# Moving a job's masks behind the final transposes, and a projection from the inverse into the carry, in a hybrid RWKV-7 and attention layer

## The chip, the cores and the metric

The kernel runs on one core of one Trainium2 chip. The metric is device time in microseconds (us) of one execution; the time before is the median of three runs.

## The reference

One layer of a diffusion backbone works on two groups of tokens, 512 latent tokens (a grid of width 64) and 128 context tokens, 640 in all, with a model width of 1024, in float32. What matters for the change is the RWKV-7 branch:

```python
h = _rmsnorm(x, p["norm1_g"]) * (1.0 + sc1) + sh1
u_rw, u_na, gate_rw, gate_na = jnp.split(h @ p["w_in"], IN_SPLITS, axis=-1)
...
u = u + mu[0] * (prev - u) + mu[1] * (nxt - u)          # centred shift in time
r, k, v, wd, ad, gd = jnp.split(u, RW_SPLITS, axis=-1)
...
def _wkv_step(s, inp):                                   # forward and backward, 8 heads of 64
    r, w, k, v, a, b = inp
    sa = jnp.einsum("bhvk,bhk->bhv", s, a)
    s = s * w[:, :, None, :] + sa[..., None] * b[:, :, None, :] + v[..., None] * k[:, :, None, :]
    return s, jnp.einsum("bhvk,bhk->bhv", s, r)
...
merged = (jax.nn.sigmoid(gate_rw) * (o_rw @ p["w_o_rwkv"])
          + jax.nn.sigmoid(gate_na) * (o_na @ p["w_o_na"]))
```

Each of r, k and v is a projection of h, shifted in time with its neighbours. The scan is computed in chunks of 64 tokens, which needs for each chunk the inverse of a triangular 64 x 64 matrix. After the branch come the output projection and a feed-forward block, which the change leaves alone.

## The kernel before

Tokens lie along the free dimension (640), channels along the partitions. The RWKV width of 512 is worked through in four channel tiles of 128, that is two heads at a time (`ct` 0 to 3). A tile has 20 lines: 10 chunks of 64 tokens in each of two directions, lines 0 to 9 forward and 10 to 19 backward. Lines 0 to 7 and 12 to 19 belong to the latent tokens, 8 to 11 to the context tokens.

A tile goes through these stages:
- `main`: for all lines the product of AG (the normalised keys with their decay) and BK gives the triangular matrices Nt (L1125).
- `inv`: DVE inverts all 20 lines at once. It transposes 32 x 32 blocks into RL, does 30 elimination steps `s` on them (L1235 to L1253), and transposes the result twice, into RT (L1262) and T (L1264). PE then multiplies with them (L1273, L1287), ACT and DVE copy the result into Rt (L1281, L1292). In steps named by `PRM["jobs"]` three jobs are put in, each for one part of the lines: `v_job` and `t_job` transpose v and BK with small matmuls (L1172, L1195), and `g_job` multiplies BK with AG and R_ (L1144, L1147; L1184 flips v for the backward lines). What a `g_job` leaves in PSUM is masked by DVE in a later step named by `PRM["mds"]`: two multiplications into AG (L1156) and two into TG (L1159). A later `g_job` for lines 12 to 19 reads v lines that the job for lines 0 to 7 has written.
- `carry`: eight slots `s` pass the state from chunk to chunk, in three phases each: AG times ZV (L1321) and a copy x0 by ACT; Rt times x0 (L1348) and a copy into ZV by ACT; TG times ZV (L1361, L1378) and a product with the decay into ZV by DVE (L1373), on which the next slot waits.
- `out`: normalisation, bonus and gating of the tile; it is woven into the next tile's inverse.

All this is latency, so PE's large matmuls are woven in. A queue of units, in the order of `PRM["order"]`, yields one fill matmul at a time (L196): k, r and v of the four tiles, 16 gates g, three low-rank projections l, then the merges a and b. Each of k, r, v, l and g has 48 matmuls, in two halves of 24. `PRM["plan"]` states for each yield of each stage how many fill matmuls follow it. The plan's stages here are inverses of 37 yields and carries of 26. PE, ACT, DVE and GpSimd run in the order that the program writes; only SyncE's order is chosen by the scheduler.

What follows a half is delayed by `later` and counted down by `tick`, one for a fill matmul and two for a yield. A gate's half is followed by a tanh on ACT and a DMA. A projection's first half is followed by a copy into the tile U, its second by another copy (`u_out`) and by the shift: an ACT operation and two DVE operations (L521, L523) for the context's 128 tokens and the same for the latent 512. U has one buffer in this stage, and its memset on GpSimd (L506) opens each projection.

During a carry the due work is held (`hold`) and given out by `beside`, which takes for each yield a budget of ACT and DVE time: work that is due goes first, then steps of `prep` for the next tile (decays, NK, BK: L599 to L688). At slot 7, `last` drains what is left of `prep`, asks for r and v of the next tile, and forms its AG (L1104) and R_ (L1107). Units wait for marks: r of a tile for the bonus of the tile before (`R`), v for the end of its inverse (`I`), k for `M`, set in `last`.

Weights come in float32 and are split into a high part by ACT (L170) and a low part, here on GpSimd in four pieces (L175).

Of the kernel before, what the change touches and what calls it, by code (L numbers as in the profile page):

```python
# [24 lines left out]
TCARGS = dict(schedule_with_timeline_sim=True)  # L25

PRM = dict(
    order=("l0 l1 k0 r0 v0 l2 g0 g1 g2 k1 g3 r1 g4 g5 v1 g6 g7 k2 r2 g8 g9 v2 g10 g11 k3 r3 g12 g13 v3 g15 g14 a0 a1 a2 a3 a4 a5 a6 a7 "
     "b0 b1 b2 b4 b3 b5 b6 b7"),
    plan=(  # L30
        "22.0 0.0 2.0 4.0",
        ("0.0.0 2.0.0 2.0.1 10.0.0 2.0.0 2.0.1 2.0.1 2.0.1 2.0.1 2.0.1 10.0.0 2.0.0 2.0.0 10.0.0 2.0.0 2.0.0 "
# [35 lines left out]
        "w >hb >lb",  # L68
        ""),
    fp=(6, 12, 18), h2e="dpddddpddd", x0e="a", ze="aa", y2=1, y1=0, sc=3, sr=3, sp=1, mg=1.915, h1=0.952,  # L70
    h2=0.91, jobs=((2, 9, 16), (2, 9, 16), (2, 9, 16), (2, 11, 16)),
    mds=((4, 11, 19), (4, 11, 19), (4, 11, 19), (4, 13, 19)), bud=((1.8, 0.8), (1.3, 1.8)), off=6, tk=2, h3=1,
    h4=1.07, g1=2, km="dddddddd", kb="ddpd", ma="d", yo="pppp", r0="pd", rl=(0, 0, 0), lh=(0, 0, 1, 1),
    wl="dddddddddppppppppppppppppppppppppppdpppppppppppp", nu=9, na=(
        "6.0.12.0.1 6.0.12.0.0 6.0.12.0.0 6.0.12.0.2 6.0.12.0.0 6.0.12.0.2 6.0.12.0.0 6.0.12.0.2 6.0.12.0.0 "
        "6.0.12.0.2 6.0.12.1.0 6.1.12.1.2 6.2.12.2.0 6.1.12.2.2 6.0.12.2.0 6.1.12.1.2 6.2.14.2.0 "
        "6.2.14.1.2 6.2.14.2.0 6.2.14.2.0 6.3.18.2.0 10.0.10.0.0"))
# [24 lines left out]
def V(ap, dims, off=0):  # L102

    return bass.AP(ap.tensor, ap.offset + off, [list(ap.ap[0])] + [list(d) for d in dims])
# [3 lines left out]
def body(ctx: ExitStack, tc: tile.TileContext, xs, xp, cols, consts, w_ada, b_row, w_rw, w_qkv,  # L108
# [26 lines left out]
    def nm(s):  # L135
        cn[0] += 1
        return f"{s}_{cn[0]}"
# [8 lines left out]
    def col(n, i=0, rows=slice(0, P)):  # L146
        return C[rows, CO[n] + i:CO[n] + i + 1]
# [40 lines left out]
    def feat_gen(ps, chunk, act_hl, nk, t0, t1, width=128, wcol=0, k0=0):  # L188

        hi, lo = chunk  # L190
        xh, xl = act_hl
        n = 0
        for kt in range(nk):
            a = kt * width + wcol
            for (w, x) in ((hi, xh), (hi, xl), (lo, xh)):
                pe.matmul(ps[:, :t1 - t0], w[:, a:a + 128], x[:, k0 + kt, t0:t1],  # L196
                          start=n == 0, stop=n == 3 * nk - 1)
                n += 1
                yield
# [90 lines left out]
    def dcol(o, i=0, rows=slice(0, P)):  # L290
        return D[rows, o + i:o + i + 1]
# [183 lines left out]
    pend, off, hold = [], [0], [False]  # L475

    def later(fn, cost=(0.5, 0), more=0):
        if off[0]:
            pend.append([off[0] + more, cost, fn])
        else:  # L480
            fn()
# [21 lines left out]
    def proj_gen(ci, out, ps_, usb, utag, ubufs, w):  # L503
        U = usb.tile([P, 643], F32, tag=utag, bufs=ubufs, name=nm("U"))
        pool.memset(V(U[:, :], [[513, 2]]), 0.0)
        pool.memset(U[:, 642:643], 0.0)  # L506
        ps0 = ps_()
        yield from feat_gen(ps0, w, (hh, hl), 8, 0, H2)
        later(lambda: act.copy(U[:, 1:321], ps0[:, :H2]))
        ps1 = ps_()  # L510
        yield from feat_gen(ps1, w, (hh, hl), 8, H2, NT)

        def u_out():
            act.copy(U[:, 321:513], ps1[:, 0:192])
            act.copy(U[:, 514:642], ps1[:, 192:320])  # L515

        def shift(a, b, u):
            o = out[:, a:b]
            n = b - a
            act.activation(o, U[:, u:u + n], AF.Identity, scale=dcol(dm, ci))  # L520
            dve.scalar_tensor_tensor(out=o, in0=U[:, u - 1:u - 1 + n], scalar=col("mu0", ci),  # L521
                                     in1=o, op0=ALU.mult, op1=ALU.add)
            dve.scalar_tensor_tensor(out=o, in0=U[:, u + 1:u + 1 + n], scalar=col("mu1", ci),  # L523
                                     in1=o, op0=ALU.mult, op1=ALU.add)

        later(u_out, (0.6, 0))
        later(lambda: shift(512, 640, 514), (0.4, 0.7), 2)
        later(lambda: shift(0, 512, 1), (0.8, 1.5), 5)

    def proj_shift(ci, out, ps_, usb, utag, ubufs):  # L530
        for _ in proj_gen(ci, out, ps_, usb, utag, ubufs, wload(w_rw[ci])):
            pass
# [159 lines left out]
    gtag = ["fl"]  # L692

    def lora_gen(i, w):

        yield from proj_gen(12 + i, lg_, flps, sb, "U", len(gtag), w)

        def two(d):
            rr, ro = slice(64 * d, 64 * d + 64), slice(64 - 64 * d, 128 - 64 * d)
            act.copy(LX[i][d][rr, :], lg_[rr, :])  # L700
            dve.tensor_tensor(out=LX[i][d][ro, :], in0=lg_[rr, :], in1=LX[i][d][rr, :].bitcast(F32),
                              op=ALU.subtract)

        if i == 2:
            later(lambda: act.activation(lg_, lg_, AF.Tanh, scale=0.5), (0.8, 0), 8)
            later(lambda: dve.tensor_scalar(out=lg_, in0=lg_, scalar1=0.5, scalar2=0.5, op0=ALU.mult, op1=ALU.add),
                  (0, 0.5), 12)
            return
        if i == 0:
            later(lambda: act.activation(lg_, lg_, AF.Tanh), (0.8, 0), 8)  # L710
        for d in range(2):
            later(lambda d=d: two(d), (0.8, 0.8), 12 + 6 * d)
# [6 lines left out]
    def unit(g, e):  # L719

        i, eng = int(g[1:]), eng_of(e)
        if g[0] in "ab":
            return 24 if g[0] == "a" else 18, lambda: merge_load(g[0], i), \
                lambda wt: merge_cast(*wt, eng), lambda w: merge_gen(g[0], i, w)
        if g[0] == "g":
            return 48, lambda: wdma(w_rw[15 + i]), lambda w: wcast(w, eng), \
                lambda w: gate_gen(i, w, flps, sb, gtag[-1])
        ci, dst = {"k": (4 + i, kt_), "r": (i, rt_), "v": (8 + i, vp0), "l": (12 + i, lg_)}[g[0]]
        return 48, lambda: wdma(w_rw[ci]), lambda w: wcast(w, eng), \
            lambda w: proj_gen(ci, dst, flps, sb, "U", len(gtag), w) if g[0] != "l" else lora_gen(i, w)  # L730
# [302 lines left out]
    with ExitStack() as s3:  # L1033
# [76 lines left out]
        parts8 = ((0, 8), (12, 20), (8, 12))  # L1110
# [102 lines left out]

        def inv(ct, S):

            jobs, mds = dict(zip(PRM["jobs"][ct], parts8)), PRM["mds"][ct]
            RL = nk_t("RL", [P, 40, 32])[:, :32, :]
            dve.transpose(RL, V(Nt[:, 0, :], [[20, 32], [1, 32]]))

# [5 lines left out]
            masks = []  # L1225
# [36 lines left out]
            dve.transpose(RT, V(RL[:, 0, :], [[1, 32], [32, 32]]))  # L1262
            T = V(f5()[:, :], [[32, 32], [1, 32]])
            dve.transpose(T, RL)  # L1264
            Hs = nk_t("Hs", [P, 40, 32])
            lohi = [(slice(64 * h, 64 * h + 32), slice(64 * h + 32, 64 * h + 64)) for h in range(2)]
            yield 2
# [223 lines left out]
        with tc.manual_schedule(engines=FIRST):  # L1491
# [4 lines left out]
            for ct in range(4):  # L1496
# [8 lines left out]
                if ct < 3:  # L1505
                    prep_dma(ct + 1, S2, sb.tile([P, NT], F32, tag="mx", bufs=2, name=nm("upw")))
                weave(inv(ct, S), (og, bg))
                drain(og)
                marks.add(f"I{ct}")
# [486 lines left out]
```

## Time and profile before

| | us |
|---|---|
| median of 3 runs | 1203.76 (1202.25 to 1204.63) |
| the profiled execution | 1201.55 |
| its span, first to last instruction | 1199.8 |
| PE busy | 1128.0 (94%) |
| DVE busy | 793.3 (66%) |
| ACT busy | 503.6 (42%) |
| GpSimd (POOL) busy | 273.8 (23%) |

The mean granted clock of TensorE is 0.985 of full speed. In the span the four tiles take from about 250 to 690 us: inverses at 266, 365, 469 and 576 us, the carries behind them. PE's busy time is an average over stages; how much of each stage it stood idle, and for whom, is read from the windows and waits.

### The profile page before, as it was taken

What the parts mean: (1) busy time and instruction counts of PE and PEld (TensorE: products, weight loads), DVE (VectorE), ACT (ScalarE), POOL (GpSimd) and SP (SyncE); (2) the same over time, 40 slices, a digit from 0 to 9 for tenths busy, and PEclk for the clock granted to TensorE, in tenths of its full rate; (3) what the DMA queues carried; (4) which work ended last, traced back from release to release, by engine and by line L of the source; (5) the groups of instructions that cost most, each with busy time, mean ns of one, the idle gap of its engine ahead of it and who ended that gap; (6) DMA issues with size and microseconds to landing.
All of it is one profiled execution on the core that took longest, in us unless ns stands there. A gap on an engine that the chain in (4) does not pass through costs nothing.

```text
span 1199.8 us, 26920 instructions
## 1 busy us (share of the span) xinstructions
PE 1128.0 (94%) x11160; PEld 999.2 (83%) x11160; DVE 793.3 (66%) x1630; ACT 503.6 (42%) x1016; POOL 273.8 (23%) x354
## 2 busy tenths in 40 slices
PE   6999999998998899899789989989999999999998
PEld 4588877788887788788778878889889989998997
DVE  4565455569558838946594684888568756875675
ACT  4444666653454364346323331754224412442240
POOL 1162244343224323342231360200001000000000
PEclk9999999999899999999899989999999999999999
DMA  9752777531211221120432571312312231222122
GB/s 336 245 115 88 238 219 231 197 124 48 66 48 37 83 69 49 54 87 29 164 129 87 177 272 54 105 36 89 106 53 88 89 105 53 89 90 90 67 73 104
DMA packets 56578, 134.48 MB, mean 112 GB/s; under 512 B 7140, under 2 KB 22116, under 8 KB 56456
## 3 DMA queue, kind: packets, MB, share of 16 engines
q1 hardware_dynamic: 55592, 131.56, 33.1%
q8 instruction: 88, 1.44, 0.5%
q10 hardware_dynamic: 864, 1.20, 0.3%
q14 instruction: 34, 0.28, 0.1%
HBM read 118.41 MB, written 14.32 MB: 111 GB/s over the span
## 4 chain that ended last, share of the span: by engine, by line
PE 61%; DVE 11%; issue 2%; ACT 2%; DMA 1%; SPq 0%; POOL 0%; DVEq 0%; ACTq 0%
PE f L1715 23%; PE acc L283 16%; PE fl L196 10%; DVE pr L1249 2%; DVE RL L1253 2%; PE w L1361 1%; PE w L1321 1%; DVE AG L1104 1%; PE w L1333 1%; PE w L1348 1%; PE mm L196 1%; PE w L1147 1%; DMA tr<-trw_d 1%; PE w L1378 1%; DVE f L1262 1%
## 5 line engine op out<-in xcount | busy, mean ns | idle before, releaser
L196 PE MATMUL fl<-h,whi 128*128 128x320 f32 x704 | 170.4, 323 | 1.9 <-ACT U L515 1.0
L175 POOL TENSOR_TENSOR wlo<-wst,whi 128x256 fp32r<-128x256 f32 x118 | 102.8, 899 | 192.1 <-ACT whi L170 188.7
L1715 PE MATMUL f<-t,whi 128*128 128x320 f32 x640 | 141.4, 309 | 0.0
L1715 PE MATMUL f<-b,whi 128*128 128x320 f32 x608 | 136.4, 312 | 3.6 <-ACT b L185 1.8
L283 PE MATMUL acc<-whi,u 128*128 128x512 f32 (+1 forms) x448 | 135.9, 385 | 0.0
L196 PEld LDWEIGHTS fl<-h,whi 128*128 128x128 f32 x704 | 121.1, 192 | 6.8 <-ACT U L515 1.2
L170 ACT CAST whi<-wst 128x1024 fp32r<-128x1024 f32 (+2 forms) x86 | 81.8, 956 | 83.2 <-PE acc L283 32.9
L196 PE MATMUL fl<-h,wlo 128*128 128x320 f32 x352 | 114.6, 326 | 0.0
L1715 PEld LDWEIGHTS f<-t,whi 128*128 128x128 f32 x640 | 107.0, 188 | 0.0
L1715 PEld LDWEIGHTS f<-b,whi 128*128 128x128 f32 x608 | 102.8, 190 | 4.7 <-ACT b L185 2.2
L1770 POOL TENSOR_TENSOR ws<-wst 128x512 f32<-128x512 f32 x20 | 27.4, 1372 | 342.0 <-DVE wlo L1759 226.2
L1715 PE MATMUL f<-t,wlo 128*128 128x320 f32 x320 | 98.9, 309 | 0.0
L283 PEld LDWEIGHTS acc<-whi,u 128*128 128x128 f32 x448 | 83.5, 188 | 16.6
L1715 PE MATMUL f<-b,wlo 128*128 128x320 f32 x304 | 94.6, 311 | 1.4 <-DVE wlo L1759 1.4
L1756 ACT CAST whi<-ws 128x1024 fp32r<-128x1024 f32 x40 | 42.0, 1050 | 108.7 <-PE f L1715 48.5
L283 PE MATMUL acc<-wlo,u 128*128 128x512 f32 (+1 forms) x224 | 86.3, 385 | 0.0
L175 DVE TENSOR_TENSOR wlo<-wst,whi 128x1024 fp32r<-128x1024 f32 (+1 forms) x49 | 61.6, 1267 | 36.5 <-ACT whi L170 36.0
L283 PE MATMUL acc<-whi,h 128*128 128x512 f32 x240 | 78.7, 402 | 1.4 <-DVE h L397 1.4
L196 PEld LDWEIGHTS fl<-h,wlo 128*128 128x128 f32 x352 | 67.8, 193 | 2.6
L1555 DVE SCALAR_TENSOR_TENSOR tt<-acc,G 128x512 f32<-128x512 f32 (+1 forms) x51 | 34.7, 681 | 51.0 <-PE acc L283 51.0
L196 PE MATMUL mm<-h,whi 128*128 128x320 f32 x288 | 65.5, 315 | 0.0
L196 PE MATMUL fl<-o,whi 128*128 128x320 f32 x224 | 56.3, 331 | 7.1 <-DMA o<-o_d 4.8
(332 smaller groups left out, 2562.1 us busy)
## 6 DMA issues: line engine op xcount, KB each, us to landing
wst<-in_w_dram SPq DMA_DIRECT2D x66, 512.0 KB
wst<-in_w_rw_dram SPq DMA_DIRECT2D x31, 512.0 KB
wa<-in_w_ada_dram SPq DMA_DIRECT2D x24, 512.0 KB
f<-in_w_ada_dram SPq DMA_DIRECT2D x16, 512.0 KB
wst<-in_w_qkv_dram SPq DMA_DIRECT2D x12, 512.0 KB
o<-o_d SPq DMA_DIRECT2D x14, 320.0 KB
x<-in_xs_dram SPq DMA_DIRECT2D x8, 512.0 KB
wa<-in_w_ada_dram SPq DMA_DIRECT2D x16, 256.0 KB
```

What stands on the lines that cost most here:

```text
L170: act.copy(hi[:, :n], st[:, :n])
L175: eng.tensor_tensor(out=lo[:, a:b], in0=st[:, a:b], in1=hi[:, a:b].bitcast(F32), op=ALU.subtract)
L196: pe.matmul(ps[:, :t1 - t0], w[:, a:a + 128], x[:, k0 + kt, t0:t1], start=n == 0, stop=n == 3 * nk - 1)
L283: pe.matmul(pss[i][:, a:b], lhs(x, kt, ts_), w[:, cs_], start=ki == 0 and n == 0, stop=ki == last and n == 2)
L1104: dve.tensor_tensor(out=AG[rr, c, h, :], in0=c64(S.kk[rr, :], d), in1=S.P65[d][rr, :, 0:64], op=ALU.mult)
L1147: pe.matmul(pr[h][hrows[h ^ i], o_], x[hrows[h], :], R_[hrows[h], l, :], start=True, stop=True)
L1249: dve.tensor_tensor(out=prv, in0=V(RL[:, s + 1 + a, :], [[32, b - a], [0, s]], s), in1=V(RL[:, s, :], [[0, b - a], [1, s]]), op=ALU.mult)
L1253: dve.tensor_tensor(out=dst, in0=dst, in1=prv, op=ALU.add)
L1555: dve.scalar_tensor_tensor(out=tt, in0=ps[:, a:b], scalar=c, in1=G[:, g, sl], op0=ALU.mult, op1=ALU.mult)
L1715: pe.matmul(ps[:, :H2], w_[:, c_], x_[:, kt, :], start=first and kt + n == 0, stop=last and kt == 3 and n == 2, skip_group_check=more)
L1756: act.copy(r[0][:, :width], src())
L1770: eng_x(PRM["se"][i - 1]).tensor_tensor(out=o_, in0=x, in1=y, op=op)
```

## The change

Three things are changed.
- The jobs take the parts of the lines in another order (`jo`): lines 8 to 11 first, 0 to 7 second, 12 to 19 third. The third job moves from step 16 to step 28, the second job's masks move from step 11 to 12 (13 to 14 in the last tile), and the third job's masks no longer have a step: they are run behind the second transpose.
- In the order of the fill, for each of the tiles 1 to 3 the projection r moves behind the gates, next to v; for tiles 2 and 3 k moves one gate forward. The plan's numbers stay.
- Outside the attention stage, the shift of the 512 latent tokens is done in two halves of 256, the second three ticks later.

```diff
-    order=("l0 l1 k0 r0 v0 l2 g0 g1 g2 k1 g3 r1 g4 g5 v1 g6 g7 k2 r2 g8 g9 v2 g10 g11 k3 r3 g12 g13 v3 g15 g14 a0 a1 a2 a3 a4 a5 a6 a7 "
-     "b0 b1 b2 b4 b3 b5 b6 b7"),
+    order=("l0 l1 k0 r0 v0 l2 g0 g1 g2 k1 g3 g4 g5 r1 v1 g6 k2 g7 g8 g9 r2 v2 g10 k3 g11 g12 g13 r3 v3 g15 g14 a0 a1 a2 "
+     "a3 a4 a5 a6 a7 b0 b1 b2 b4 b3 b5 b6 b7"),
...
-    h2=0.91, jobs=((2, 9, 16), (2, 9, 16), (2, 9, 16), (2, 11, 16)),
-    mds=((4, 11, 19), (4, 11, 19), (4, 11, 19), (4, 13, 19)), bud=((1.8, 0.8), (1.3, 1.8)), off=6, tk=2, h3=1,
+    h2=0.91, jobs=((2, 9, 28), (2, 9, 28), (2, 9, 28), (2, 11, 28)),
+    mds=((4, 12), (4, 12), (4, 12), (4, 14)), bud=((1.8, 0.8), (1.3, 1.8)), off=6, tk=2, h3=1,
...
+    nu=9, jo=(2, 0, 1), na=(
...
-        later(lambda: shift(0, 512, 1), (0.8, 1.5), 5)
+        if len(gtag) > 1:
+            later(lambda: shift(0, 512, 1), (0.8, 1.5), 5)
+        else:
+            later(lambda: shift(0, 256, 1), (0.4, 0.8), 5)
+            later(lambda: shift(256, 512, 257), (0.4, 0.8), 8)
...
-            jobs, mds = dict(zip(PRM["jobs"][ct], parts8)), PRM["mds"][ct]
+            jobs, mds = dict(zip(PRM["jobs"][ct], (parts8[i] for i in PRM["jo"]))), PRM["mds"][ct]
...
             T = V(f5()[:, :], [[32, 32], [1, 32]])
             dve.transpose(T, RL)
+            for f in masks:
+                f()
```

`gtag` has two entries in the attention stage and one afterwards.

More of the change, by code (lines that the diff above doesn't have):

```diff
@@ L70 @@
     fp=(6, 12, 18), h2e="dpddddpddd", x0e="a", ze="aa", y2=1, y1=0, sc=3, sr=3, sp=1, mg=1.915, h1=0.952,
-    h2=0.91, jobs=((2, 9, 16), (2, 9, 16), (2, 9, 16), (2, 11, 16)),
-    mds=((4, 11, 19), (4, 11, 19), (4, 11, 19), (4, 13, 19)), bud=((1.8, 0.8), (1.3, 1.8)), off=6, tk=2, h3=1,
+    h2=0.91, jobs=((2, 9, 28), (2, 9, 28), (2, 9, 28), (2, 11, 28)),
+    mds=((4, 12), (4, 12), (4, 12), (4, 14)), bud=((1.8, 0.8), (1.3, 1.8)), off=6, tk=2, h3=1,
     h4=1.07, g1=2, km="dddddddd", kb="ddpd", ma="d", yo="pppp", r0="pd", rl=(0, 0, 0), lh=(0, 0, 1, 1),
-    wl="dddddddddppppppppppppppppppppppppppdpppppppppppp", nu=9, na=(
+    wl="dddddddddppppppppppppppppppppppppppdpppppppppppp", nu=9, jo=(2, 0, 1), na=(
         "6.0.12.0.1 6.0.12.0.0 6.0.12.0.0 6.0.12.0.2 6.0.12.0.0 6.0.12.0.2 6.0.12.0.0 6.0.12.0.2 6.0.12.0.0 "
```

## The prediction

> **What bounds the kernel now.** I read the page's table of engines first, then the busy time by stage of the recurrence, then who waited for whom on PE, window by window.
>
> ```profile
> PE 1128.0 (94%) x11160; PEld 999.2 (83%) x11160; DVE 793.3 (66%) x1630; ACT 503.6 (42%) x1016; POOL 273.8 (23%) x354
> ```
>
> PE is the bound over the whole, and the change gives it not one matmul more or less: it can only win or lose the idle time of PE. The six windows below are inverse, carry, inverse, carry, inverse, carry of the first three channel tiles. The columns are the window, its length, busy time (and instructions) of PE, PE's weight loads, DVE, ACT and POOL, the granted clock, and DMA.
>
> ```profile
> 266.00:304.00 38.00, 31.85 (x688) 30.38 (x683) 37.04 (x133) 13.90 (x32) 10.61 (x20) 0.95 0.14 47
> 312.00:361.00 49.00, 47.00 (x631) 41.03 (x629) 23.84 (x41) 26.77 (x71) 15.49 (x20) 1.00 0.18 58
> 365.00:412.00 47.00, 38.86 (x720) 35.53 (x717) 42.75 (x141) 19.27 (x43) 18.80 (x27) 0.97 0.16 58
> 417.00:466.00 49.00, 47.47 (x719) 42.07 (x720) 25.51 (x42) 25.82 (x70) 16.43 (x22) 1.00 0.18 58
> 469.00:513.00 44.00, 37.90 (x728) 35.02 (x728) 41.01 (x139) 17.15 (x38) 16.67 (x25) 0.99 0.16 54
> 519.00:572.00 53.00, 51.06 (x726) 44.81 (x728) 26.01 (x46) 27.87 (x75) 14.81 (x23) 1.00 0.16 55
> ```
>
> The reader sees two regimes: in an inverse DVE is busy 37.0 of 38 us, 42.8 of 47 and 41.0 of 44, and PE idles 6 to 8 us; in a carry DVE is busy about half, and PE idles 1.5 to 2 us. The waits on PE say where (total us, times, longest), in windows around the final transposes of inverses 0, 1, 2 and 3:
>
> ```profile
> PE w L1273 <- DVE f L1262: 5.3, 1, 5.3
> ...
> PE w L1273 <- DVE f L1262: 3.3, 1, 3.3
> PE fl L196 <- ACT U L515: 1.0, 1, 1.0
> PE fl L196 <- ACT U L509: 0.9, 1, 0.9
> ...
> PE w L1273 <- DVE f L1262: 3.7, 1, 3.7
> ...
> PE fl L196 <- DVE mt L1461: 2.0, 2, 1.4
> PE w L1273 <- DVE f L1262: 0.2, 1, 0.2
> ```
>
> L1262 is the first of two transposes that end DVE's chain of 30 elimination steps; L1273 are the matmuls that need it. PE has spent its woven fill by then and stands still.
>
> **Step 1, the masks of the third job.** A job's masks are two AG multiplies (L1156) and two TG multiplies (L1159). DVE's groups in inverse 0, two jobs of eight lines (512 elements) and one of four (256):
>
> ```profile
> L1156 DVE TENSOR_TENSOR AG<-w,K 64x512 f32<-64x512 f32 x4 | 2.8, 689 | 0.1
> L1159 DVE TENSOR_TENSOR TG<-w,K 128x512 f32<-128x512 f32 x4 | 2.5, 673 | 0.0
> ...
> L1156 DVE TENSOR_TENSOR AG<-w,K 64x256 f32<-64x256 f32 x2 | 0.8, 422 | 0.0
> ...
> L1159 DVE TENSOR_TENSOR TG<-w,K 128x256 f32<-128x256 f32 x2 | 0.7, 406 | 0.0
> ```
>
> An eight-line job's masks are (2.8 + 2.5) / 2 = 2.65 us, the four-line job's 1.5. Before, 6.8 us of masks stand ahead of L1262. After, the four-line job comes first, then lines 0 to 7, and lines 12 to 19 last, with masks behind the second transpose: 4.15 us stand ahead, so L1262 comes 2.65 us earlier. Queued behind the moved masks on DVE are the copies into Rt, for which PE waits in the carry's second matmul group (L1348). In inverses 0 to 2 r's shift, 2.2 us by step 2, stands in just that place now and goes, so against the transposes the copies come 0.45 later; L1262 coming earlier by more covers that, and uncovered it would be 0.45 each.
>
> **Step 2, the order of the fill.** The plan pulls a fixed number of fill matmuls at each yield, 48 to a unit. Counted from the end of the attention stage, the pulls of main, inverse and carry 0 are 1-28, 29-193 and 194-325; of tile 1, 326-353, 354-517 and 518-644. Before, r1 holds pulls 97-144 and r2 433-480, both inside inverses, and their shifts fall right around the transposes. After, r1 holds 193-240 and r2 529-576, in the carries just ahead of v, and gates stand in their place; k2 moves from 385-432 to 337-384, early in its inverse. Tile 2 is alike. No unit comes ahead of the mark it waits for, so no pull is lost. With r ahead of v, v's memset of U (L506) stands on POOL until r's last half shift has read U; behind it are the memset of a P65 column and the next unit's low weights, which PE wants five yields later or more. I cost that at nothing; uncovered, the nearest row is the 0.9 of L509 above, where r2's copy waited for U behind k2's shift. The gates' DMAs only leave SyncE at other moments, and the merge reads them much later. A gate puts one ACT tanh and a DMA behind each half; a projection puts on DVE two operations of each of these sizes:
>
> ```profile
> 399.95 0.34 DVE L521 SCALAR_TENSOR_TENSOR kt__620<-U,C,kt__620 128x128 f32<-128x128 f32 x1
> ...
> 401.21 0.74 DVE L521 SCALAR_TENSOR_TENSOR kt__620<-U,C,kt__620 128x512 f32<-128x512 f32 x1
> ```
>
> That is 2 x 0.34 + 2 x 0.74 = 2.2 us per shift. Halving the 512 costs a fixed part: linear between the sizes, 256 elements take 0.47 us, so four of them take 1.9 in place of 1.5, 0.4 us more per projection (k, r and v of three tiles). k stays ahead of L1262 and pays its 0.4 there: 2.65 - 0.4 = 2.25 us net. DVE also waited for PE inside inverses 1 and 2 (window over both):
>
> ```profile
> DVE bv L1095 <- PE w L1093: 2.7, 3, 2.0
> ...
> DVE AG L1156 <- PE w L1144: 1.9, 2, 1.5
> ```
>
> The second line is masks waiting for their job's matmuls; a first job of half the size and a second mask one step later (12 for 11) should remove it, 1.9 us, in inverse 1. The 2.0 lies in inverse 2 behind the first job, and I take 1.4 of it as gone.
>
> **Step 3, what each inverse gains.** PE wins what L1262 comes earlier, up to what it waited. A long wait also costs afterwards: windows before a wait, after the 5.3 and after the 3.3 (third value PE's matmuls, clock third from the end).
>
> ```profile
> 286.00:296.00 10.00, 10.00 (x70) 10.00 (x70) 9.96 (x48) 4.11 (x8) 4.05 (x4) 1.00 0.27 96
> 304.00:307.10 3.10, 3.10 (x12) 3.10 (x13) 3.00 (x6) 1.95 (x5) 0.00 (x0) 0.50 0.32 74
> 410.20:412.70 2.50, 2.50 (x13) 2.50 (x10) 2.45 (x5) 1.67 (x4) 0.00 (x0) 0.50 0.00 0
> ```
>
> At clock 1.00 ten us hold 68 to 70 matmuls, 0.147 each; at 0.50 half the pace. So 3.1 and 2.5 us at half rate lose 1.5 and 1.2.
> - Inverse 0: -2.2 (5.3 to about 3.1; nearest row 3.3, so the half rate stays).
> - Inverse 1: 2.25 + 1.9, say -4.1, out of 3.3 + 1.0 + 0.9 of waiting; the 0.9 goes with r2. With about 1 us of wait left the half rate goes, -1.2.
> - Inverse 2: 2.25 + 1.4, -3.6 out of 3.7, and -1.2.
> - Inverse 3: no r, no half rate. Its 2.0 us of waits on mt came of merges queued behind the old third masks; but the new ones delay the merge at a4's second half and the Rt copies by 2.65, so I take half, -1.0.
>
> Sum -13.3. Between ends: masks less k's split alone, -2.2 three times and -0.2, is -6.8; all the waits and half rates quoted, -20.
>
> **Step 4, what the carries lose.** In a carry a budget meters the preparation of the next tile onto ACT and DVE; a shift that is due goes first and pushes preparation back. What has not been metered by slot s = 7 is drained at once, ahead of AG (L1104), for which PE waits when the next tile begins. DVE is then the bound already:
>
> ```profile
> 449.93 0.83 DVE L679 TENSOR_TENSOR f<-NK,pre 128x640 f32<-128x640 f32 x1
> 450.86 0.82 DVE L664 SCALAR_TENSOR_TENSOR NK<-pre,kk 128x640 f32<-128x640 f32 x1
> 453.58 0.61 DVE L1373 TENSOR_TENSOR ZV<-w,Dt 64x128 f32<-64x128 f32 x2 [1.89 <-PE w L1361]
> ...
> 455.69 2.19 DVE L679 TENSOR_TENSOR f<-NK,pre 128x640 f32<-128x640 f32 x1
> ```
>
> By the budgets, in carry 1 the first L679 and L664 above fall behind the last ZV product (453.58) after the change: 0.83 + 0.82, 0.4 for v's split, and 0.5 while ACT finishes NK behind them, +2.5 at AG. In carry 2 three such products (2.5) and 0.4 are added; an idle gap of 1.8 at the same place (the row below), where DVE waits for ACT's NK, shrinks by about 1.1, since DVE has other products to do by then: +1.8. In carry 0 only one product changes place and the halved v shift lets the ZV product go sooner; I take +0.5 for the middle of the carry, where r's shift stands ahead of one ZV product.
>
> ```profile
> 560.87 0.83 DVE L669 TENSOR_TENSOR NK<-NK,kt__620 128x640 f32<-128x640 f32 x1 [1.78 <-ACT NK L662]
> ```
>
> Carries 1 and 2 then end in 3 to 4 us of waiting, near the 3.3 that brought the half rate: half a chance of 1.2 each, +1.2 together. Sum +6.0; ends: +1 if the idle half of DVE takes up all of it, +13.5 if each of three carries loses r's split shift (2.2 + 0.4), v's split (0.4) and a half rate (1.5).
>
> **The sum.** -13.3 + 6.0 = -7.3 us. The profiled execution took 1201.55 us with a span of 1199.8; the median of three runs is 1203.76. So 1194.2 for a profile like this one, and 1196.5 for the median. Runs spread from 1202.25 to 1204.63, so 0.2%, 2.4 us, is about what can be told from no change.
>
> **The rivals.** A: the carries cover nothing. r's shift lands whole in front of AG in all three (+13.5), against inverses midway between -6.8 and -13.3, -10: +3.5, 1207.3. It decides, by more than 2.4 us, from 12.4 us of cost at AG against -10, from 9.2 against -6.8. For it: every carry already ends with PE waiting on DVE. Against it: 24 to 26 us of DVE work in 49 to 53. Chance 0.12.
>
> B: the idle time covers nearly all (+1): -12.3, 1191.5. For it the same windows; against it that AG ends a chain, not a sum. Chance 0.22.
>
> C: DVE's gain ahead of L1262 is the masks alone (-6.8), and the carries cost 6: -0.8, 1203.0, no change to be told. Chance 0.11.
>
> D: DVE and POOL collide more often. POOL's add (455.12, 2.07) ran under the L679 at 455.69, whose twin at 449.93 took 0.83:
>
> ```profile
> 455.12 2.07 POOL L688 TENSOR_TENSOR bv<-bv,NK 128x640 f32<-128x640 f32 x1 [9.81 <-PE w L1321]
> ```
>
> Were each of three r shifts to meet a split on POOL and lose 1.36 (2.19 - 0.83), 4.1 us go: -3.2, 1200.6. Chance 0.05. The Trainium skill, "SBUF — State Buffer", section "Who interferes with whom", says that a DVE instruction with two SBUF inputs contends with a GpSimd one that reads SBUF, the later being blocked outright; shifts are of that kind, masks with one input in PSUM are not. By that rule the row above is a block, and the trace agrees as far as 1.36 us goes.
>
> My forecast has 0.50. Faster by over 0.2%: forecast, B and D, 0.77; within: C, 0.11; slower: A, 0.12. The range leaves A out and holds the others with 1 to 2 us around B and C, whose terms are no surer than the rest: 1190 to 1205.
>
> **What would show it.** Right: L1273's wait falls to about 3 us in inverse 0 and under 1.5 in 1 and 2; the clock stays at 1.00 after those two; the ACT U waits of 1.0 and 0.9 go; the wait of L1125 for AG grows to 3 to 4 us in carries 1 and 2 and hardly in carry 0. Wrong: L1273 still waits 3 us in inverse 1 (DVE's waits for PE were not removed), a new wait on Rt or x0 at L1348, or waits for ZV (L1321) in the middle of carries.

## The result and the profile after

The changed kernel takes 1217.65 us (median of five, 1215.75 to 1220.12) against 1203.48 for the kernel before on the same chip (1200.61 to 1204.63): a ratio of 1.0116 (95% interval 1.0101 to 1.0131), 14.0 us slower. The forecast was 1196.5, faster. The profiled execution after took 1220.12 us with a span of 1218.0, the longest of its five; before it was 1201.55, near the short end of its own. So the traces lie 18.2 us apart, some 4 more than the medians, and shares read from them are read with that in mind.

PE's matmuls are the same 11160, and are now busy longer (1128.0 us before):

```profile
PE 1136.8 (93%) x11160; PEld 1008.4 (83%) x11160; DVE 806.8 (66%) x1648; ACT 505.4 (41%) x1025; POOL 260.5 (21%) x354
```

To lay stages beside each other I cut both traces at the same three instructions of each tile: the first matmul of main (L1125 before, L1129 after), the first that needs the transposes (L1273, L1279) and the first of the carry (L1321, L1327). From one to the next, after minus before in us:

| tile | main and inverse | final matmuls, Rt | carry |
|---|---|---|---|
| 0 | +0.9 | +0.1 | +1.4 |
| 1 | +2.8 | -1.3 | +2.3 |
| 2 | +3.6 | -0.8 | +0.7 |
| 3 | +4.2 | +2.9 | +0.3 |

(The last carry is taken to the end of the kernel; 1.3 of the 18.2 lie ahead of the first main, where no instruction differs.) The carries lose 4.4 in the first three tiles, where 6.0 was forecast. The inverses, which were to gain 13.3, lose. Their windows from main to transposes, for the four tiles, first before, then after; the columns are those of the windows in the prediction (third value PE's busy time, clock third from the end):

```profile
262.00:302.30 40.30, 34.18 (x790) 32.45 (x790) 37.01 (x132) 16.20 (x33) 12.80 (x24) 0.97 0.20 65
360.40:408.80 48.40, 39.82 (x816) 35.82 (x817) 42.90 (x139) 20.03 (x41) 23.40 (x31) 1.00 0.17 58
463.00:510.80 47.80, 40.18 (x817) 36.61 (x816) 42.51 (x140) 18.89 (x38) 16.36 (x27) 1.00 0.17 61
569.30:627.90 58.60, 47.53 (x844) 42.38 (x843) 41.60 (x147) 17.25 (x35) 14.59 (x20) 0.94 0.44 152
```

```profile
263.30:304.50 41.20, 34.36 (x794) 32.42 (x794) 37.84 (x130) 15.19 (x31) 12.06 (x24) 0.98 0.27 84
364.00:415.10 51.10, 41.76 (x812) 38.26 (x811) 44.45 (x141) 19.23 (x39) 15.00 (x23) 0.90 0.18 60
470.50:521.80 51.30, 43.12 (x816) 39.17 (x816) 46.33 (x145) 18.88 (x39) 13.87 (x21) 0.90 0.17 56
580.20:643.10 62.90, 49.38 (x847) 45.01 (x848) 42.78 (x143) 16.31 (x32) 12.51 (x20) 0.84 0.40 137
```

Two things are read here. In inverses 1 to 3 the same matmuls are busy 1.9, 2.9 and 1.9 us longer, while the granted clock fell from 1.00, 1.00 and 0.94 to 0.90, 0.90 and 0.84 (at 0.50 a matmul takes nearly twice as long, as the windows in the prediction show). And DVE, from whose chain 2.65 us of masks were taken in each, is busy longer in all four. What PE waits for in inverse 0, 1, 2 and 3 after the change (us in total, times, longest; each row for its own inverse alone):

```profile
PE w L1279 <- DVE f L1266: 6.0, 1, 6.0
...
PE w L1151 <- DVE out L1415: 5.3, 2, 3.3
PE w L1188 <- DVE out L1404: 2.2, 1, 2.2
...
PE w L1151 <- DVE out L1415: 5.3, 2, 3.3
PE w L1129 <- DVE AG L1108: 2.6, 4, 0.9
...
PE fl L196 <- DVE mt L1467: 5.7, 1, 5.7
PE fl L196 <- DMA o<-o_d: 5.2, 2, 4.2
```

In inverses 1 and 2 the wait for the transposes (3.3 and 3.7 before) is gone, as forecast. A new wait stands earlier, at L1151: these are the matmuls of the job at step 28, and what releases them is DVE reading a result of `out` (L1415), the block of the previous tile that is woven into this inverse. The chain in inverse 1, on DVE and then on PE:

```profile
383.09 0.35 DVE L521 SCALAR_TENSOR_TENSOR kt__620<-U,C,kt__620 128x128 f32<-128x128 f32 x1 [4.21 <-ACT kt__620 L520]
...
396.30 0.68 DVE L1404 TENSOR_TENSOR out<-out,w 128x512 f32<-128x512 f32 x1
...
402.76 0.48 DVE L1415 TENSOR_TENSOR out<-w,out 128x320 f32<-128x320 f32 x1
```

```profile
397.03 0.33 PE L1188 MATMUL w<-ZV,J 64*64 64x64 f32 x4 [2.17 <-DVE out L1404]
...
400.88 0.47 PE L1151 MATMUL w<-R__2889,f 64*64 64x64 f32 x2 [3.33 <-DVE out L1415]
...
403.29 0.38 PE L1151 MATMUL w<-R__2889,f 64*64 64x64 f32 x3 [1.94 <-DVE out L1415]
```

The last job needs six `w` buffers, and there are six in all; up to four still hold what `out` has computed and DVE has not yet read. PE takes its instructions in order, so it stands there, with its fill queued behind. In inverse 1 DVE is late with k2: moved one gate forward, its shift stands at a point of DVE's chain that PE's matmuls have not reached, 4.21 us of idle time. In inverse 2 DVE idles only 0.2 us ahead of k3's shift, and PE waits the same 5.3 at L1151, so what makes DVE late there stays open. The windows of the stretch in inverse 1 show the price on the clock:

```profile
396.00:400.00 4.00, 0.53 (x8) 0.39 (x8) 3.76 (x16) 0.92 (x1) 0.00 (x0) 0.77 0.00 0
400.00:404.00 4.00, 1.18 (x29) 0.99 (x33) 4.00 (x19) 1.19 (x4) 1.19 (x2) 0.50 0.00 0
404.00:408.00 4.00, 4.00 (x108) 3.88 (x103) 4.00 (x10) 3.13 (x6) 3.56 (x5) 0.50 0.56 206
```

The second cause shows in inverse 0, where no `out` runs. DVE and POOL after the change:

```profile
285.47 1.27 DVE L1163 TENSOR_TENSOR TG<-w,K 128x512 f32<-128x512 f32 x2
286.67 1.37 DVE L1253 TENSOR_TENSOR pr<-RL 128x117 f32<-128x117 f32 x2
287.96 1.53 DVE L1257 TENSOR_TENSOR RL<-RL,pr 128x117 f32<-128x117 f32 x2
289.42 0.46 DVE L1253 TENSOR_TENSOR pr<-RL 128x112 f32<-128x112 f32 x2
...
296.82 0.94 DVE L1253 TENSOR_TENSOR pr<-RL 128x72 f32<-128x72 f32 x2
297.68 1.47 DVE L1257 TENSOR_TENSOR RL<-RL,pr 128x72 f32<-128x72 f32 x2
```

```profile
278.56 3.07 POOL L175 TENSOR_TENSOR wlo<-wst,whi 128x256 fp32r<-128x256 f32 x4 [8.69 <-PE w L1151]
286.42 2.94 POOL L175 TENSOR_TENSOR wlo<-wst,whi 128x256 fp32r<-128x256 f32 x4 [4.79 <-ACT whi L170]
296.67 3.06 POOL L175 TENSOR_TENSOR wlo<-wst,whi 128x256 fp32r<-128x256 f32 x4 [7.31 <-ACT whi L170]
```

A pair of elimination steps that takes 0.46 us takes 1.37 and 1.53 while POOL splits weights, and 0.46 again when the split has ended. I took, for each pair, what it lasted over the shortest pair of the same shape in any of the traces, and summed that in the four inverses: 3.7, 3.0, 3.0 and 0.6 us before, 10.2 in all (rounded parts), and 6.0, 5.7, 3.0 and 3.9 after, 18.6. In inverse 0 that eats 2.3 of the 2.65 us of masks. I call these blocks below. (Which pairs count as one shape moves these sums by a few tenths.)

### The profile page after: what moved, and what is told of

The parts are those of the page before. It is cut to its first block, busy times and chain, and to the rows that moved or that the text cites. A ratio compares the mean times of both kernels' runs of the same rounds, so it can differ in the third digit from the quotient of the medians.

```text
span 1218.0 us, 26953 instructions
## 1 busy us (share of the span) xinstructions
PE 1136.8 (93%) x11160; PEld 1008.4 (83%) x11160; DVE 806.8 (66%) x1648; ACT 505.4 (41%) x1025; POOL 260.5 (21%) x354
## 4 chain that ended last, share of the span: by engine, by line
PE 62%; DVE 11%; ACT 2%; DMA 2%; issue 1%; SPq 0%; POOL 0%; DVEq 0%; ACTq 0%
PE f L1721 22%; PE acc L283 16%; PE fl L196 12%; DVE pr L1253 2%; DVE RL L1257 2%; PE w L1327 1%; PE w L1367 1%; PE w L1339 1%; PE w L1354 1%; PE w L1151 1%; PE mm L196 1%; PE w L1384 1%; DMA tr<-trw_d 1%; PE w L1345 1%; PE w L1129 1%
## 5 line engine op out<-in xcount | busy, mean ns | idle before, releaser
L175 POOL TENSOR_TENSOR wlo<-wst,whi 128x256 fp32r<-128x256 f32 x118 | 90.7, 798 | 161.8 <-ACT whi L170 149.8
L283 PEld LDWEIGHTS acc<-whi,u 128*128 128x128 f32 x448 | 83.5, 188 | 16.7
L196 PE MATMUL fl<-o,whi 128*128 128x320 f32 x224 | 59.3, 345 | 13.3 <-DVE mt L1467 5.7
```

The costliest lines, as they stand in the source:

```text
L175: eng.tensor_tensor(out=lo[:, a:b], in0=st[:, a:b], in1=hi[:, a:b].bitcast(F32), op=ALU.subtract)
L283: pe.matmul(pss[i][:, a:b], lhs(x, kt, ts_), w[:, cs_], start=ki == 0 and n == 0, stop=ki == last and n == 2)
```

## The experiments

**One part at a time.** Four kernels, each the kernel before with one part of the change.

Jobs only (the `jobs`, `mds`, `jo` and late-mask lines of the diff above):

> Before with the jobs, their order and the late masks alone; order of the fill and shift as before. Theory T (PE, which runs its instructions in order, meets at the job of step 28 the w buffers that the block of out still holds, and is tied to DVE there): most of the loss is here, +8 to +12 us; in inverses 1 and 2 PE waits 4 to 5.5 us at L1151 for DVE's L1415, and the wait of PE for the final transposes is near 0 in both. Rival R (the loss is the new order of the fill: r in the carries and k2 early): -7 to 0 us, the gain of the moved masks, and no wait at L1151 over 1 us. In inverse 0, where no out runs, both theories expect what the changed kernel showed, a wait for the transposes of 5 to 6 us.

Order only (the two `order` lines):

> Before with the new order of the fill alone; jobs, masks and shift as before. Theory T: the carries' loss of 3 to 5 us and no more, +2 to +5 us in all, less what the waits for U of 1.9 us give back; DVE idles about 4 us for k2's projection in inverse 1 without much harm. Rival R: +8 to +14 us.

Split only (the `shift` lines):

> Before with the halved shift of 512 alone. By the sizes 0.4 us more of DVE per projection of nine, of which only those ahead of the transposes or of AG show: 0 to +2 us by theory T and by rival R. A third theory, that the halves meet POOL's weight splits more often and are blocked: +3 us and more.

Order of the jobs without the step 28:

```diff
-    mds=((4, 11, 19), (4, 11, 19), (4, 11, 19), (4, 13, 19))
+    mds=((4, 12, 19), (4, 12, 19), (4, 12, 19), (4, 14, 19))
-            jobs, mds = dict(zip(PRM["jobs"][ct], parts8)), PRM["mds"][ct]
+            jobs, mds = dict(zip(PRM["jobs"][ct], (parts8[i] for i in (2, 0, 1)))), PRM["mds"][ct]
```

> Before with the small job first (lines 8-11, 0-7, 12-19) and the second job's masks one step later, the third job still at step 16 and its masks at step 19. Theory T (the step 28 is what harms, not the order of the jobs): -3 to +1.5 us, no wait at L1146 (the t_job's matmuls) for out over 1 us, and DVE's wait for PE at the masks of inverse 1 (1.9 us) gone. If the order of the jobs is itself the harm: +5 us and more.

| kernel | ratio to before | 95% interval | us |
|---|---|---|---|
| jobs only | 0.9970 | 0.9952 to 0.9988 | -3.6 |
| order only | 1.0097 | 1.0075 to 1.0120 | +11.7 |
| split only | 1.0020 | 1.0006 to 1.0033 | +2.4 |
| job order, third job at 16 | 0.9981 | 0.9966 to 0.9995 | -2.3 |

(The us, here and below, are the ratio less one times 1204.) My first theory, that the jobs are the loss, fell: alone they gain, PE waits only 2.0 and 2.9 us at the job of step 28 in inverses 1 and 2, and inverse 1 is 5.7 us shorter in that trace. Their new order without the step 28 does no harm either. The split's +2.4 (0.7 to 4.0) lies between the 0 to 2 by its sizes and the 3 and more of the third theory, and decides between them no further. The loss is in the order of the fill; but the three parts add up to 10.5 us, and the whole change costs 14.0, so they also act on each other. Next, the order's own halves.

r1, r2 and r3 alone moved next to v:

```diff
-... g3 r1 g4 g5 v1 g6 g7 k2 r2 g8 g9 v2 g10 g11 k3 r3 g12 g13 v3 ...
+... g3 g4 g5 r1 v1 g6 g7 k2 g8 g9 r2 v2 g10 g11 k3 g12 g13 r3 v3 ...
```

> Before with r1, r2 and r3 alone moved behind their gates, next to v; k2 and k3 where they were. Theory K (the loss of the order is k's earlier place: its shift stands early in DVE's chain, where DVE still runs ahead of PE and so waits): the carries' loss alone, +2 to +5 us, and inverses 1 and 2 within 2 us of before. Theory R (taking r out of the inverses and into the carries is itself the loss): +8 to +13 us.

k2 and k3 alone one gate earlier:

```diff
-... g3 r1 g4 g5 v1 g6 g7 k2 r2 g8 g9 v2 g10 g11 k3 r3 g12 g13 v3 ...
+... g3 r1 g4 g5 v1 g6 k2 g7 r2 g8 g9 v2 g10 k3 g11 r3 g12 g13 v3 ...
```

> Before with k2 and k3 alone one gate earlier in their inverses; r where it was. Theory K: +6 to +10 us, 4 to 5 us more in each of inverses 1 and 2, with DVE idle about 4 us for k2's copy in inverse 1. Theory R: -1 to +3 us.

r alone: 1.0085 (1.0065 to 1.0106), +10.2 us. k alone: 1.0033 (1.0015 to 1.0051), +4.0. So theory K, that k's place is most of it, is wrong too, though DVE does idle 4.8 us for k2 there. With r moved, the carries lose 3.5 in the trace, as forecast; the rest lies in inverses 1 and 2 (+5.0, +3.8), and 3.3 of it are new blocks in inverse 1 (6.3 against 3.0).

**Blocks taken away and doubled.** The splits of the woven units left out on GpSimd, once with before's order, once with the new order, later with the whole change. In their place ACT copies the weights, which puts about 20 us more on ACT over the kernel (503.6 to 523.1), while GpSimd's busy time falls from 273.8 to 196.3:

```diff
         step = 256 if eng is pool else n
+        if eng is pool and rec:
+            act.copy(lo[:, :n], st[:, :n])
+            return hi, lo
```

> Before, with GpSimd's splits of the woven projections' and gates' weights left out: ACT writes a plain copy of the weights as their low halves, so r, k, v and the gates are not the reference's; the times of the other work stay. Theory P (GpSimd's splits block DVE's two-input elimination steps, and the order decides how often they meet): the steps of 1.4 to 1.5 us all go to 0.35 to 0.5, -3 to -8 us. Theory K (what counts is where DVE waits for PE): -3 to +1 us, since DVE's steps are not what sets the end.

> The new order of the fill alone, with the same splits left out as in the run before it. Theory P: its distance to the run with before's order shrinks from 12.7 us to the carries' 3 to 5. Theory K: it stays 10 to 13 us, and DVE still idles 4 us for k2's copy in inverse 1.

> The whole change, with GpSimd's splits of the woven projections' and gates' weights left out as above (a plain copy by ACT for the low halves, so r, k, v and gates are not the reference's). Theory P (most of the change's loss is blocks of DVE's steps by these splits): against before with the same splits left out, -4 to +4 us instead of +14, the rest being the carries (+4) and inverse 3 (+5) against the moved masks (-5 to -8). Theory T (PE tied to DVE by the w buffers at step 28, and k's early place): +9 to +14 us, the splits having no part in it.

And in before, each split written twice:

```diff
-        for a in range(0, n, step):
+        for a in [*range(0, n, step)] * (2 if rec and eng is pool else 1):
```

> Before, with each of GpSimd's splits of the woven units written twice, the same values. Theory P: DVE's blocked elimination steps (10.2 us over their shortest in the four inverses before) grow to 16 to 22, and the time by +5 to +11 us. Theories T and K: PE does not wait for these low halves, so -1 to +2 us.

| kernel | ratio to before | 95% interval | blocks, us |
|---|---|---|---|
| before, no splits | 0.9903 | 0.9880 to 0.9925 | 4.3 |
| order only, no splits | 0.9937 | 0.9920 to 0.9954 | 4.4 |
| whole change, no splits | 0.9985 | 0.9970 to 1.0000 | 7.2 |
| before, splits twice | 1.0115 | 1.0094 to 1.0136 | 19.9 |

PE's wait for the transposes in inverse 0, without the splits and with the splits twice (5.3 before):

```profile
PE w L1276 <- DVE f L1265: 2.0, 1, 2.0
```

```profile
PE w L1273 <- DVE f L1262: 10.3, 1, 10.3
PE fl L196 <- POOL wlo L175: 1.2, 1, 1.2
```

And with the splits twice in inverse 1, where the wait for the transposes (3.3 before) is gone:

```profile
PE fl L196 <- POOL wlo L175: 2.2, 1, 2.2
PE fl L196 <- ACT U L515: 2.1, 1, 2.1
```

The dose answers in both directions, and by more than expected, -11.7 us without and +13.8 with two. The doubled splits do not act through blocks alone: PE itself waits 3.4 us for low halves, which the expectation had ruled out, and 3.0 for U in place of 1.9. Without splits the order alone costs 0.9937 - 0.9903, 4.1 us (give or take 3.4, from the intervals), in place of 11.7: theory P's forecast for the order came in, and about 7.6 us of its loss go with the splits. How is not shown: the order-only trace has only some 3 us more of blocks than before, most of it in inverse 2, while its inverses 1 and 2 lose 5.3 and 4.9. Nor are the 4.1 us shown to be the carries': the two traces without splits differ by 2.1 in the first three carries and by 4.8 in the inverses (the one with before's order is the shortest of its six executions). For the whole change theory P does not suffice: 0.9985 - 0.9903 is still 9.9 us, beyond the 4 that I expected at most, and PE still waits 4.9 and 4.0 us at the job of step 28 in inverses 1 and 2.

**The fourth tile.** The new jobs in three tiles (`jobs`, `mds` and `jo` by tile, the last tile as before), and in the second tile alone, with before's order and shift:

```diff
+    ... jobs=((2, 9, 28), (2, 9, 28), (2, 9, 28), (2, 11, 16)),
+    mds=((4, 12), (4, 12), (4, 12), (4, 13, 19)), ... jo=((2, 0, 1), (2, 0, 1), (2, 0, 1), (0, 1, 2)), ...
```

> Before with the new jobs, their order and the late masks in the first three tiles alone; order of the fill, shift and the fourth tile as before. If the fourth tile's loss in the jobs-only run (5.5 us, PE waiting 5.7 for the merge's add and 1.5 for its second) is the merge queued behind the second and third masks there: 4 to 6 us faster than jobs only, -7 to -10 against before. If it was that execution's lateness of a DMA: the same as jobs only, -3 to -4.

> The new jobs in the second tile alone, the only one whose inverse and carry together got shorter in the jobs-only run (-5.7 - 1.2 + 1.6). By those stages: -4 to -6 us. If the loss of tiles 0 and 2 was chance and their masks do help: less than the run with three tiles, -2 to -3.

Three tiles: 0.9925 (0.9899 to 0.9951), -9.0 us; one tile: 0.9939 (0.9921 to 0.9957), -7.3, more than the stages had promised. The fourth tile alone costs 0.9970 - 0.9925, 5.4 us. Its waits with the new jobs there, and without:

```profile
PE fl L196 <- DMA o<-o_d: 5.9, 2, 4.0
PE fl L196 <- DVE mt L1463: 5.7, 1, 5.7
PE fl L196 <- DVE P L1463: 1.5, 1, 1.5
```

```profile
PE fl L196 <- DMA o<-o_d: 5.0, 2, 4.0
PE fl L196 <- DVE mt L1463: 2.0, 2, 1.4
```

In that tile the fill is the merge, whose two `fl` buffers DVE must read. The 1.5 is a read (P) that now stands behind the third masks. The 5.7 is a read behind the second masks, where it stood before too; but before, PE ran the third job's matmuls in that time (606.1 to 609.7 us in the trace before), and with that job at step 28 it has none. The three-tile kernel is faster than both kernels of this study.

**The tie at step 28.** The whole change with the old order; then the whole change with the results of `out` copied to SBUF by ACT, first where they are used (called e14 in an expectation below), on the three-tile kernel too, then ahead of everything that waits for DVE:

> The whole change with before's order of the fill (new jobs and late masks in all tiles, halved shifts). If the parts add up: -3.6 + 2.4, -1 us (-4 to +2), and the order is the 13 to 15 us that are missing to the change. If the loss needs jobs and split together and not the order: +6 to +12 us.

```diff
-            dve.tensor_tensor(out=yc[:, :512], in0=yc[:, :512], in1=pa[:, :512], op=ALU.mult)
-            dve.tensor_tensor(out=yc[:, 512:], in0=yc[:, 512:], in1=pb[:, :128], op=ALU.mult)
+            oc = ysq
+            act.copy(oc[:, :512], pa[:, :512])
+            act.copy(oc[:, 512:], pb[:, :128])
+            dve.tensor_tensor(out=yc, in0=yc, in1=oc, op=ALU.mult)
...
+                act.copy(oc[:, hs_], ps[:, :H2])
...
-                dve.tensor_tensor(out=yc[:, hs_], in0=ps[:, :H2], in1=yc[:, hs_], op=ALU.mult)
+                dve.tensor_tensor(out=yc[:, hs_], in0=oc[:, hs_], in1=yc[:, hs_], op=ALU.mult)
```

> The whole change, with the results of out (the two halves of the broadcast and the two of the gate) copied by ACT into SBUF, so that their w buffers come free without DVE; four copies more on ACT. Theory T (PE tied to DVE by these buffers costs what it waits): the waits of 5.3 in inverses 1 and 2 fall under 2, and the time from +14 to +4 to +9. If the tie only moves a wait that the transposes would have cost: PE waits there instead at the transposes, and the time stays at +12 to +15.

> The new jobs in three tiles (old order, whole shifts) with the same copies of out's results. There PE waits 2.0 and 2.9 us for out in inverses 1 and 2. Theory T: 2 to 5 us less than without the copies, -10 to -13 against before. Otherwise -7 to -10, as without.

```diff
+            og = pre_t()
+            for hf in range(2):
+                hs_ = slice(hf * H2, (hf + 1) * H2)
+                ps = wps()
+                pe.matmul(ps[:, :H2], S.gup, lg_[:, hs_], start=True, stop=True)
+                act.copy(og[:, hs_], ps[:, :H2])
             dve.tensor_tensor(out=yc, in0=yc, in1=ysq, op=ALU.mult)
```

> The whole change, with out's gate matmuls and the copies of all four of its results put ahead of the activation that waits for DVE. Theory T (the tie is a cost): no wait of PE at L1151 over 1.5 us in inverses 1 and 2, and +2 to +8 us against before, where the whole change has +14 and e14 +9.8. Rival (PE only waits elsewhere, for the transposes or for out's other results): L1279 waits 3 us and more again in inverses 1 and 2, and +9 to +14 us.

The whole change with the old order: 1.0022 (1.0008 to 1.0037), +2.6, just above the -4 to +2 of adding the parts; so the order's share inside the whole change is 11.3 us. The first copies: 1.0081 (1.0062 to 1.0099). They did not undo the tie: ACT's two copies of the gate's results stand behind an activation and a cast that themselves wait for DVE (8.0 and 2.4 us in inverse 1), and PE waited for ACT instead, 6.2 us in inverse 1:

```profile
PE w L1151 <- ACT pre L1416: 6.2, 2, 3.5
```

On the three-tile kernel the same copies did nothing, 0.9928 (0.9907 to 0.9950). With the copies ahead (inverses 1 and 2):

```profile
PE fl L196 <- ACT fl L546: 4.0, 1, 4.0
PE w L1082 <- ACT pre L1077: 1.6, 1, 1.6
...
PE w L1129 <- DVE AG L1108: 2.6, 4, 0.9
PE fl L196 <- ACT fl L546: 1.8, 1, 1.8
```

No wait at L1151 or at the transposes is left, 4.0 and 1.8 us wait for a gate's tanh on ACT (L546), and the two inverses are 3.4 and 5.1 us shorter than after. The ratio is 1.0056 (1.0035 to 1.0076): the tie costs 1.0116 - 1.0056, 7.2 us, of the whole change. It takes both the job at step 28 and the new order: with the old order PE waits 2.0 and 2.2 us at L1151 in the two inverses, and on the three-tile kernel the first copies gained nothing. The copies ahead were not run with the old order, so that they would gain nothing there is argued, not shown.

**All three away.** The whole change with the tie undone, the fourth tile's jobs as before and the splits left out:

> The whole change with the tie undone as in the run before it, the fourth tile's jobs as before's, and GpSimd's splits of the woven units left out (plain copies by ACT, so r, k, v and gates are not the reference's). Against before with the same splits left out (0.990 of before): if these three are all that harms, the carries' +4 is left against the masks' -5 to -8, so -4 to +1 us from that (0.987 to 0.991 of before). If something else is at work: over 0.994.

0.9887 (0.9870 to 0.9904), against 0.9903 for before without splits: 1.9 us faster, inside the expected band, though with these intervals not to be told from no difference. The account: tie 7.2, fourth tile 5.4, splits 4.1 (they cost the whole change 1.0116 - 0.9985, 15.8 us, and before 11.7), together 16.7, and -1.9 for the rest: +14.8 against +14.0 measured. By the intervals each of the four terms is known to 3 or 4 us, and the fourth tile's was measured without the new order, so that the sum comes within 0.8 is partly luck. That the three together are the whole loss is what the last kernel shows, to within 3.4 us.

**A better version still?** The three-tile kernel with the splits of r1, g4 and g5 (these three, where the expectation lists them loosely) on DVE, one operation of 1.2 us each:

```diff
-    wl="dddddddddpppppp...
+    wl="dddddddddppdddp...
```

> The new jobs in three tiles with the splits of the three units that are cast in inverse 0 (g4, g5 and the one after r1) on DVE, one operation of about 1.3 us each in place of four on GpSimd. Theory P: the 6.9 us of blocked steps in inverse 0 go, 3.9 of splits come, 2 to 3 us less wait for the transposes and -10 to -12 in all. Otherwise the splits only add their 3.9 to DVE's chain: -4 to -6 in all.

0.9917 (0.9893 to 0.9941), -10.0: the blocks of inverse 0 fall from 6.9 to 0.4 and its wait to the row below, but 3.6 us come back in carry 0, and the time can't be told from the three-tile kernel's, so the gain that theory P expected did not show.

```profile
PE w L1275 <- DVE f L1262: 1.6, 1, 1.6
```

## Why the prediction was wrong

**Step 3 failed**, the gain of the inverses: -13.3 forecast, between -6.8 and -20; measured +11.4 in the traces up to the transposes, +12.3 with the final matmuls. "PE wins what L1262 comes earlier, up to what it waited" was the sentence. It was wrong in three ways.
- In inverses 1 and 2 the wait at the transposes did go, and I had named that as the sign of being right. But PE's wait moved, to L1151. I priced the third job only by its masks on DVE, and never asked which `w` buffers its matmuls find at step 28, though `out` was in the same inverse: 7.2 us by the runs.
- The half rate, which I had credited with -1.2 twice, came back: after the new waits the clock stands at 0.50 for 404 to 408 us above.
- L1262 did not come 2.2 us earlier in inverse 0, since the blocks took 2.3 and the halved k shift had its own (one half 1.00 us long in place of 0.48). Without the splits the term was right: there the change shortens inverse 0 by 2.1 and the matmuls behind it by 1.3.

In inverse 3 I took -1.0 and had seen the merge behind the new third masks as the risk. The runs say +5.4. The mishap I named was the case, but as a wait of 1.5; the larger wait, 5.7, comes, as the two traces read, of the third job's matmuls no longer standing where PE waits for the merge's read, which the sum does not have at all.

**Step 2** priced k's move one gate forward at nothing. It put 4.21 us of DVE idle time into inverse 1, and k alone cost 4.0. In the whole change this idle time counts by way of the tie: with the tie undone it is still 4.21, and inverse 1 is 0.6 us shorter than before. DVE's wait for PE at the masks of inverse 1, 1.9, went as forecast. The waits for U of 1.0 and 0.9 did go, as forecast; the halved shift was priced at 0.4 per projection and measures +2.4 over all, within the 3.6 of nine projections.

**Step 1**'s sizes hold, 1.39 and 1.27 for the masks in the new place.

**Step 4**, the carries: +6.0 forecast, +4.4 measured, with 1.4, 2.3 and 0.7 against my 0.5, 2.5 and 1.8; the half rate did not come there. The waits for AG grew to 2.6 and 2.7 ahead of tiles 2 and 3, not to 3 to 4.

Of the rivals, A had the sign, but by a cost of 13.5 in the carries, which lost 4.4. D had the mechanism of the blocks, but only for r's shifts in the carries, and still forecast a gain. The blocks are in the inverses. The splits cost 11.7 us before and 15.8 after, so the change added 4.1 (give or take 3.7); that D's 4.1 is the same figure is chance. The Trainium skill, "SBUF — State Buffer", section "Who interferes with whom", says that issue order and not the shape of the operation decides who blocks. The traces agree in that either side can be the one that waits, and this is what I had missed. Before, in inverse 1, a split began among back-to-back steps, and it was POOL that had to wait:

```profile
384.07 7.59 POOL L175 TENSOR_TENSOR wlo<-wst,whi 128x256 fp32r<-128x256 f32 x4 [6.25 <-ACT whi L170]
```

```profile
388.44 0.46 DVE L1253 TENSOR_TENSOR RL<-RL,pr 128x108 f32<-128x108 f32 x2
388.82 0.67 DVE L1398 TENSOR_TENSOR out<-out,w 128x512 f32<-128x512 f32 x1
389.42 0.27 DVE L1399 TENSOR_TENSOR out<-out,w 128x128 f32<-128x128 f32 x1
389.62 1.46 DVE L1249 TENSOR_TENSOR pr<-RL 128x114 f32<-128x114 f32 x2
391.00 0.99 DVE L1253 TENSOR_TENSOR RL<-RL,pr 128x114 f32<-128x114 f32 x2
```

The steps ran at 0.46 until DVE came to two operations that read PSUM (L1398, L1399); then POOL was in (its first piece took 5.43 us, the other three 0.74 to 0.77), and the next steps took 1.46 and 0.99. In the changed kernel's inverse 0 the split of 286.42 began during masks, which read PSUM, and it was the steps behind them that took longer. But the split of 296.67, shown above too, began among back-to-back steps and was not held off: it took 3.06, and the steps 0.94 and 1.47. So masks and shifts at another place of DVE's chain can change which splits block it, a cost that no duration of a moved operation contains; they are not all that decides it. That this is why one order blocks more than another is my reading of these rows, and not shown; what is shown is that most of the order's loss goes with the splits.

What stays open: how the splits make the order dear beyond the blocks that I counted; why DVE is late in inverse 2; and how the 10.2 us of r alone divide, beyond the 3.5 of the carries and the 3.3 of blocks in inverse 1. Inverse 2 lost 3.8 there with hardly more blocks, at a granted clock of 0.93.

## What to carry to other kernels

When a job moves on an engine that runs in order, list the buffers that it takes and who still holds them at its new place, not only the engine it was meant to relieve; a wait that disappears where it was watched may stand a few instructions earlier. On a DVE chain of two-input SBUF operations beside GpSimd splits, time one run without the GpSimd work before tuning the order: here the kernel before was 11.7 us faster without it. And change one stage at a time: the same edit gained 9 us in three tiles and lost 5 in the fourth.

## What the hardware showed

A GpSimd split of four 128x256 pieces takes 2.8 to 3.1 us when it wins, and took 7.59 where DVE's back-to-back steps held it off; DVE's pair of small steps goes from 0.46 to 1.4 or 1.5 when it loses, so the small operations pay three times their length. DVE operations that read one input from PSUM kept their duration beside a split, and it kept its own. Before, in inverse 0, POOL and DVE:

```profile
280.38 2.91 POOL L175 TENSOR_TENSOR wlo<-wst,whi 128x256 fp32r<-128x256 f32 x4 [11.89 <-ACT whi L170]
```

```profile
280.53 1.39 DVE L1156 TENSOR_TENSOR AG<-w,K 64x512 f32<-64x512 f32 x2
281.85 1.27 DVE L1159 TENSOR_TENSOR TG<-w,K 128x512 f32<-128x512 f32 x2
```

The same masks take 1.39 and 1.27 in the kernel without splits.
